# Window attention: mask, maximum and copy of the scores in one VectorE instruction

## The chip, the cores and the metric

The kernel runs on one core of a Trainium2 chip. A core has a matrix engine (TensorE, PE in the profile, with its weight loads as PEld), a vector engine (VectorE, DVE), a scalar engine (ScalarE, ACT), a general engine (GpSimd, POOL) and queues that issue transfers (here SyncE's, SP). Each engine runs its own instructions in order, and they wait for each other by semaphores. Matrix products go to PSUM, the rest lives in SBUF. The metric is the device time of one execution in microseconds.

## The reference, cut to what matters

The program is one step of a small backbone of two layers on 256 context tokens and 1024 latent tokens. The change lies in the first layer's attention: 16 query heads in 4 groups that share keys and values, 64 dimensions a head. For the latent tokens each block of 128 queries sees the three blocks of 128 keys around it (two at either end), a mask that cuts this to +-128 tokens, 256 cached keys that are not masked, and a learned logit per head, the sink, which counts in the softmax but has no value:

```python
valid = (jnp.abs(qpos[:, None] - kpos[None, :]) <= WINDOW) & (kpos >= 0)[None, :] & (kpos < T)[None, :]
s_loc = jnp.einsum('bqhgd,bkhd->bhgqk', qi, ki, preferred_element_type=F32) * scale
s_loc = jnp.where(valid, s_loc, NEG_INF)
s_ctx = jnp.einsum('bqhgd,bkhd->bhgqk', qi, ck, preferred_element_type=F32) * scale
p = jax.nn.softmax(jnp.concatenate([s_loc, s_ctx, sink_b], axis=-1), axis=-1)
p_loc = p[..., :3 * BLOCK].astype(v.dtype)
p_ctx = p[..., 3 * BLOCK:3 * BLOCK + L].astype(v.dtype)
```

The context tokens attend to all 256 context keys and the sink, without a mask.

## The kernel before, in words

The attention stage handles 40 groups: 4 head groups, each with the latent blocks 0 to 7 and the context blocks 8 and 9, in the order 0, 1, 2, 8, 3, 4, 5, 9, 6, 7. A group has four heads, so there are 160 heads and blocks, 128 of them with a window. The instructions stand in the order in which the code issues them. `Attention.run` counts ticks. In one tick it normalises (`normal`) the pair of heads scored two ticks ago, takes the maximum (`peak`) of the head scored in the tick before, turns and splits one block of 128 keys of four finished heads (`turn`, `split`), multiplies the block turned before by the values (`weighted`), takes the exponential (`exp`), does a piece of other work (`extra`: projections, later the output product, tiles `mm`), and issues the score products (`scores`) of the next head. Scores are issued at least seven ticks less the head's number ahead of the group's first `turn`.

Scores go to a tile D of two PSUM banks, of which there are two. Columns 0 to 511 hold the window, right-aligned (`off` is its first column: 128 inside, 256 in blocks 0 and 7, 512 for context blocks, which have none), 512 to 767 the cached keys. Keys are held as a high and a low part, `att_kh` and `att_kl`; each part takes one product per piece. For a window a third product adds the mask: a 128x128 identity times the triangular masks, both kept in bf16 in a tile `mbf`, which is filled when startup ends. The queries' high and low part lie one above the other in `att_q`.

`peak` (L1368 and L1369) copies the head's sink to column 768 of D and takes the maximum of the columns from `off` to 768, negated, into `att_nm`. `exp` (L1374) reads D from PSUM, writes the tile `att_p` (`att_pp` for context blocks) in SBUF and adds up the denominators, `att_den`. `normal` (L1380 and L1383) inverts these and scales `att_p` on POOL. `turn` transposes `att_p` on TensorE (L123), `split` (L1394 and L1395) makes a high part `att_ph` on ScalarE and a low part `att_pl` on VectorE, and `weighted` multiplies both by `att_v` into V. `a_sinks` loads the sinks; `LR` loads the masks into `K.small` at startup.

All matrix products stand at L119 in the profile, transposes at L123, loads at L154.

Of the kernel before, what the change touches and what calls it, by code (L numbers as in the profile page):

```python
# [11 lines left out]
F32 = mybir.dt.float32  # L12
F32R = mybir.dt.float32r
BF16 = mybir.dt.bfloat16
AF = mybir.ActivationFunctionType
ALU = mybir.AluOpType
AX = mybir.AxisListType
# [34 lines left out]
def _rope_tables(n_tok, width, grid_w=64, base=10000.0):  # L52
    half = width // 4
    f32 = np.float32
    freqs = np.power(f32(base), -(np.arange(half, dtype=f32) / f32(half))).astype(f32)
    t = np.arange(n_tok)
    pos = [(t // grid_w).astype(f32), (t % grid_w).astype(f32)]
    cos = np.zeros((width, n_tok), f32)
    sin = np.zeros((width, n_tok), f32)
    for ax in range(2):  # L60
        ang = (pos[ax][None, :] * freqs[:, None]).astype(f32)
        c, s = np.cos(ang), np.sin(ang)
        r = ax * 2 * half
        cos[r:r + half] = c
        cos[r + half:r + 2 * half] = c
        sin[r:r + half] = -s
        sin[r + half:r + 2 * half] = s
    reps = 128 // width
    return np.tile(cos, (reps, 1)), np.tile(sin, (reps, 1))


def _constants():
    f32 = np.float32
    ca, sa = _rope_tables(TS, 64)
    cc, sc = _rope_tables(TS, 32)
    p = np.arange(128)[:, None]
    f = np.arange(128)[None, :]
    eye = (p == f).astype(f32)
    m_f = np.where(p <= f, 0, NEG).astype(f32)
    m_b = np.where(p >= f, 0, NEG).astype(f32)  # L80
    w_lo = np.where(f >= p, 0, NEG).astype(f32)
    w_hi = np.where(f <= p, 0, NEG).astype(f32)
    rst = np.ones((128, T), f32)
    rst[0:32, 0::128] = 0
    rst[32:64, 127::128] = 0
    return {
        "k_small": np.concatenate([eye, m_f, m_b, m_f, w_lo, w_hi], axis=1),
        "k_ropea": np.concatenate([ca, sa], axis=1),
        "k_ropec": np.concatenate([cc, sc], axis=1),
        "k_rst": rst,  # L90
    }
# [68 lines left out]
def body(tc, I, O, dbg=None, stop_at=None):  # L160
    K = Kern(tc, I, O, dbg)
    with ExitStack() as ctx:
        K.const = ctx.enter_context(tc.tile_pool(name="const", bufs=1))
        K.dram = ctx.enter_context(tc.tile_pool(name="dram", bufs=1, space=DRAM))
        K.left = lambda n: tc.alloc_tile_pool(name=n, bufs=1, side="left", reuse_waits="tile")
        K.right = lambda n: tc.alloc_tile_pool(name=n, bufs=1, side="right", reuse_waits="tile")
        K.set_psum(S=6, T=2)
        setup_consts(K)
        layer_ab(K)
        layer_c(K)  # L170
        K.set_psum()
# [35 lines left out]
def setup_consts(K):  # L207
    nc, c = K.nc, K.const
    K.ident = c.tile([128, 128], F32, tag="ident", name="ident")
    K.small = c.tile([128, 5, 128], F32, tag="small", name="small")  # L210
    K.mbf = c.tile([128, 3, 128], BF16, tag="mbf", name="mbf")
    unit = c.tile([128, 5], F32, tag="unit", name="unit")
    nc.vector.memset(unit, 0.0)
    nc.vector.memset(unit[:, 1:2], 1.0)
    K.vpad = unit[:, 1:5].rearrange("p (a e) -> p a e", a=2)
    K.sel = [unit[:, 1:3], unit[:, 0:2]]
    K.mhalf = c.tile([128, 1], F32, tag="mhalf", name="mhalf")
    nc.vector.memset(K.mhalf, -0.5)


class Startup:
# [21 lines left out]
    def run(self, order, room):  # L243
        K, nc = self.K, self.K.nc
        self.G = room
        self.by = dict(a=nc.scalar, v=nc.vector, p=nc.gpsimd)
        K.flow = self
        for token in order.split():
            name, at, by = re.fullmatch(r"([A-Za-z]+)(\d*)([avp]?)", token).groups()
            getattr(self, name)(*[int(a) for a in at], *by)  # L250
        while self.kept or self.last:
            if not self.kept:
                self.kept, self.last = self.last, []
            self.kept.pop(0)()
        K.flow = None
        nc.vector.tensor_copy(K.mbf[:, 0, :], K.ident)
        nc.vector.tensor_copy(K.mbf[:, 1:3, :], K.small[:, 3:5, :])

    def later(self, f, n):
        self.kept.append(f)  # L260
# [638 lines left out]
def layer_ab(K):  # L899
# [90 lines left out]
    with K.tc.manual_schedule():  # L990
        K.pairs = True
        beside_memory(K, bp, dense, 23, 230)
        K.pairs, K.spread = False, True
        bp.release()
        gp.release()
        K.set_psum(D=2, mm=3, V=1)
        ap = left("att")
        a_sinks(K, ap)
        K.rpool.release()
        stage = right("raw")  # L1000
        steps = beside_attention(K, ap, dense, place_wout(K, hp, w, wt, stage, [8, 9, 10, 11, 12, 13], 3),
                                 release)
# [187 lines left out]
def a_sinks(K, ap):  # L1190
    nc = K.nc
    K.sink = ap.tile([128, 16], F32, tag="sink", name="sink")
    K.dma(K.sink, K.I["sink_a"].to_broadcast([128, 16]))


def a_proj(K, wp, g):
# [119 lines left out]
class Group:  # L1316
# [27 lines left out]
    def scores(self, h):  # L1344
        K, (kh, kl), b, off, c0 = self.A.K, self.A.kk, self.b, self.off, self.c0
        S = self.D[h] = K.t(K.psum["D"], [128, 1024], F32, "D")
        q = self.q[:, h, :]
        if b < 8:
            K.mm(S[:, off:512], q, kh[:, self.k0:self.k1], True, False)
            K.mm(S[:, off:512], q, kl[:, self.k0:self.k1], False, False)  # L1350
            if b == 0:
                K.mm(S[:, 384:512], K.mbf[:, 0, :], K.mbf[:, 2, :], False, True)
            elif b == 7:
                K.mm(S[:, off:off + 128], K.mbf[:, 0, :], K.mbf[:, 1, :], False, True)
            else:
                ends = S[:, 0:512].rearrange("p (a f) -> p a f", a=2)[:, :, 128:256]
                K.mm(ends, K.mbf[:, 0, :], K.mbf[:, 1:3, :], False, True)
        K.mm(S[:, 512:768], q, kh[:, c0:c0 + 256], True, False)
        K.mm(S[:, 512:768], q, kl[:, c0:c0 + 256], False, True)

    def peak(self, h):
        K, ap, S = self.A.K, self.A.ap, self.D[h]
        if h % 2 == 0:
            P = K.t(ap, [128, 2, 648], F32, "att_p", 5) if self.b < 8 else K.t(ap, [128, 2, 264], F32, "att_pp", 2)
            self.P[h // 2] = (P, K.t(ap, [128, 2], F32, "att_nm", 4),
                              K.t(ap, [128, 2], F32, "att_den", 4))
        i = 4 * self.g + h
        K.nc.vector.tensor_copy(S[:, 768:769], K.sink[:, i:i + 1])  # L1368
        K.nc.vector.tensor_reduce(self.P[h // 2][1][:, h % 2:h % 2 + 1], S[:, self.off:769], AX.X, ALU.max, negate=True)  # L1369

    def exp(self, h):
        P, nm, den = self.P[h // 2]
        i = slice(h % 2, h % 2 + 1)
        self.A.K.nc.scalar.activation(P[:, h % 2, 0:self.w + 1], self.D[h][:, self.off:769], AF.Exp,  # L1374
                                      bias=nm[:, i], accum_out=den[:, i])

    def normal(self, pr):
        P, _, den = self.P[pr]
# [1230 lines left out]
```

## Time and profile before

| | us |
|---|---|
| median of 3 runs | 2569.25 |
| lowest and highest run | 2566.27 and 2574.26 |
| profiled execution, device time | 2568.26 |
| profiled execution, span of its instructions | 2566.5 |
| first to last score product of the stage | 1030.4 to 1426.0 |
| in that stage: TensorE, VectorE, ScalarE, GpSimd busy | 391.57, 300.24, 272.48, 213.28 |

Line numbers are those of the kernel before; from the first lines of the change on, those of the changed kernel differ by a few. In a row of groups the operands stand as out<-in with partitions x elements, then the count, the busy time and the mean of one, then the engine's idle time before them with what ended it. In rows in order of time the first number is the start, the second the duration. Matmuls overlap, and their ends are modelled, so durations of TensorE's rows cannot be added up.

### The profile page before, as it was taken

Reading aid. Unit: us, or ns where it says so; the run is one execution under the profiler, and the core shown is the slowest. Engines: PE = TensorE matmul, PEld = TensorE weight load, DVE = VectorE, ACT = ScalarE, POOL = GpSimd, SP = SyncE. Lnnn points to the kernel's source line nnn. Section 1 sums busy time; section 2 is a strip of 40 time slices with the busy share of each in tenths; the row PEclk is TensorE's granted clock in tenths of the full one; section 3 lists DMA queues with packets and bytes.
Section 4 is the critical chain, followed back from the end, with each engine's and each line's share of the span. In section 5 each row is a group of like instructions: output and inputs, shape, how many; then the busy total and the mean of one; then the engine's idle time right before and its main releaser. Section 6 shows DMA issues by size and latency. Waiting matters only on the chain.

```text
span 2566.5 us, 48614 instructions
## 1 busy us (share of the span) xinstructions
PE 2526.6 (98%) x16482; PEld 2245.1 (87%) x16482; DVE 1700.2 (66%) x3925; ACT 1438.6 (56%) x3665; POOL 1131.6 (44%) x1512
## 2 busy tenths in 40 slices
PE   8999999999999999999999999999999999999998
PEld 6898998998998888878888888898899999999887
DVE  6643655756657575687777456436888888888754
ACT  6423534535534432577666433234888888888842
POOL 6222333333325344366554543135555545555732
PEclk9999999999999999999999999999999999999999
DMA  7665576566667574465443554433211111111334
GB/s 266 212 181 175 156 219 189 170 201 186 191 207 223 171 222 147 116 175 155 126 130 94 168 164 161 126 82 110 67 35 31 39 30 41 33 32 35 115 99 133
DMA packets 338954, 347.20 MB, mean 135 GB/s; under 512 B 36409, under 2 KB 281838, under 8 KB 338450
## 3 DMA queue, kind: packets, MB, share of 16 engines
q1 hardware_dynamic: 338706, 344.10, 43.9%
q8 instruction: 131, 2.15, 0.3%
q14 instruction: 117, 0.96, 0.1%
HBM read 233.49 MB, written 110.50 MB: 134 GB/s over the span
## 4 chain that ended last, share of the span: by engine, by line
PE 87%; DVE 3%; ACT 2%; issue 1%; POOL 1%; DMA 1%; SPq 0%; POOLq 0%; DVEq 0%; ACTq 0%
PE mm L119 36%; PE S L119 29%; PE V L119 9%; PE T L123 7%; PE D L119 3%; PE mm L123 3%; PE T L119 1%; DVE cpl L2549 0%; DVE cmx L2499 0%; POOL w L1070 0%; DVE att_pl L1395 0%; DMA out_new_cache_a_k<-scr 0%; ACT att_ph L1394 0%; DVE att_nm L1369 0%; ACT cPa L2501 0%
## 5 line engine op out<-in xcount | busy, mean ns | idle before, releaser
L585 POOL TENSOR_TENSOR wl<-wf,wh 128x256 fp32r<-128x256 f32 (+2 forms) x272 | 223.0, 846 | 483.6 <-ACT wh L584 399.6
L119 PE MATMUL mm<-hTh,wh 128*128 128x512 f32 (+1 forms) x912 | 329.2, 361 | 0.9 <-DVE scr L870 0.9
L119 PE MATMUL mm<-hTh,wl 128*128 128x512 f32 (+1 forms) x912 | 324.7, 356 | 0.0
L119 PE MATMUL mm<-hTl,wh 128*128 128x512 f32 (+1 forms) x912 | 324.1, 355 | 0.0
L119 PE MATMUL S<-cK,cQ 96*128 96x512 f32 (+3 forms) x1248 | 298.2, 364 | 0.8 <-ACT cPa L2501 0.7
L2549 DVE TENSOR_TENSOR cpl<-T,cph 128x512 fp32r<-128x512 f32 x336 | 228.8, 685 | 45.2 <-ACT cph L2548 41.8
L119 PEld LDWEIGHTS S<-cK,cQ 96*128 96x128 f32 (+1 forms) x1248 | 193.5, 189 | 22.5 <-ACT cPa L2501 2.8
L2548 ACT CAST cph<-T 128x512 fp32r<-128x512 f32 x336 | 192.6, 590 | 30.2 <-PE T L123 21.2
L119 PEld LDWEIGHTS mm<-hTh,wl 128*128 128x128 f32 x912 | 171.5, 188 | 27.0
L119 PEld LDWEIGHTS mm<-hTh,wh 128*128 128x128 f32 x912 | 171.5, 188 | 23.8 <-DVE scr L870 1.1
L119 PEld LDWEIGHTS mm<-hTl,wh 128*128 128x128 f32 x912 | 171.7, 188 | 23.2
L2499 DVE TENSOR_REDUCE cmx<-S 128x1 f32<-128x512 f32 x256 | 173.2, 682 | 19.5 <-PE S L119 18.4
L1394 ACT CAST att_ph<-mm 128x512 fp32r<-128x512 f32 x168 | 98.6, 587 | 93.2 <-PE mm L123 89.9
L2480 POOL TENSOR_SCALAR cPa<-cPa,cst 128x512 f32<-128x512 f32 x128 | 99.0, 773 | 108.1 <-DVE cst L2477 91.4
L1395 DVE TENSOR_TENSOR att_pl<-mm,att_ph 128x512 fp32r<-128x512 f32 x168 | 115.8, 689 | 35.7 <-ACT att_ph L1394 30.9
L119 PE MATMUL mm<-wh,hTh 128*128 128x256 f32 x480 | 135.5, 282 | 0.0
L119 PE MATMUL mm<-wl,hTh 128*128 128x256 f32 x480 | 134.9, 281 | 0.0
L119 PE MATMUL mm<-wh,hTl 128*128 128x256 f32 x480 | 134.5, 280 | 0.0
L1383 POOL TENSOR_SCALAR att_p<-att_p,att_den 128x640 f32<-128x640 f32 (+1 forms) x128 | 97.9, 779 | 79.4 <-DVE att_den L1380 31.4
L584 ACT CAST wh<-wf 128x256 fp32r<-128x256 f32 (+2 forms) x272 | 96.0, 409 | 60.3 <-DMA wf<-in_w_in_c 29.3
L119 PE MATMUL V<-cph,cV 128*128 128x256 f32 x440 | 118.1, 289 | 1.9 <-ACT cph L2548 1.9
L1369 DVE TENSOR_REDUCE att_nm<-D 128x1 f32<-128x641 f32 (+2 forms) x160 | 114.9, 718 | 5.5
(488 smaller groups left out, 7938.9 us busy)
## 6 DMA issues: line engine op xcount, KB each, us to landing
wf<-in_w_in_ab SPq DMA_DIRECT2D x120, 256.0 KB, 3.8
in<-in SPq DMA_DIRECT2D x40, 514.0 KB, 3.5
in<-in SPq DMA_DIRECT2D x32, 386.0 KB, 3.8
mw<-in_w_mod SPq DMA_DIRECT2D x48, 256.0 KB, 4.7
in<-scr SPq DMA_DIRECT2D x40, 258.0 KB, 3.6
o_x<-y SPq DMA_DIRECT2D x20, 512.0 KB, 3.5
xin<-in_k_wmod SPq DMA_DIRECT2D x16, 512.0 KB, 7.9
in<-cx SPq DMA_DIRECT2D x32, 256.0 KB, 3.5
```

The costliest lines, as they stand in the source:

```text
L119: return self.nc.tensor.matmul(out, lhsT, rhs, start=start, stop=stop)
L123: self.nc.tensor.transpose(out, in_, self.ident[:p, :p])
L584: K.nc.scalar.copy(wh, wf[:, k])
L585: K.nc.gpsimd.tensor_sub(wl, wf[:, k], wh.bitcast(F32))
L1369: K.nc.vector.tensor_reduce(self.P[h // 2][1][:, h % 2:h % 2 + 1], S[:, self.off:769], AX.X, ALU.max, negate=True)
L1383: nc.gpsimd.tensor_scalar(pv, pv, den[:, i:i + 1], 1.0, ALU.mult, ALU.mult)
L1394: K.nc.scalar.copy(ph, self.T)
L1395: K.nc.vector.tensor_sub(pl, self.T, ph.bitcast(F32))
L2480: nc.gpsimd.tensor_scalar(pv, pv, wt[:, c:c + 1], rd, ALU.mult, ALU.mult)
L2499: nc.vector.tensor_reduce(mx[:, b, c:c + 1], S, AX.X, ALU.max, negate=True)
L2548: nc.scalar.copy(ph, T_)
L2549: nc.vector.tensor_sub(pl, T_, ph.bitcast(F32))
```

## The change

The mask product on TensorE and its bf16 tile go away. A mask in f32, laid out as the scores are (two triangles and zeros in five blocks of 128 columns), is loaded once into SBUF when the stage begins, and the sinks are negated there. In `peak` one VectorE instruction reads the scores from PSUM and the mask from SBUF, writes minus their sum to `att_p`, and keeps the minimum of these, starting from the negated sink; a second instruction of the pair stores that minimum in `att_nm`. The negated sinks are copied into the column behind the scores, for two heads at a time. `exp` then works on `att_p` in place, with a factor of -1. Block 7 has its two window blocks in another place than the others, so it reads the mask in two pieces. Context blocks go through the same instruction with the zero part of the mask.

```diff
         "k_small": np.concatenate([eye, m_f, m_b, m_f, w_lo, w_hi], axis=1),
+        "k_mask": np.concatenate([w_lo, 0 * eye, w_hi, 0 * eye, 0 * eye], axis=1),
...
-    K.mbf = c.tile([128, 3, 128], BF16, tag="mbf", name="mbf")
...
-        nc.vector.tensor_copy(K.mbf[:, 0, :], K.ident)
-        nc.vector.tensor_copy(K.mbf[:, 1:3, :], K.small[:, 3:5, :])
...
     K.dma(K.sink, K.I["sink_a"].to_broadcast([128, 16]))
+    K.mask = ap.tile([128, 768], F32, tag="mask", name="mask")
+    K.dma(K.mask[:, 0:640], K.I["k_mask"])
+    nc.vector.tensor_scalar(K.sink, K.sink, -1.0, None, ALU.mult)
...
             K.mm(S[:, off:512], q, kh[:, self.k0:self.k1], True, False)
-            K.mm(S[:, off:512], q, kl[:, self.k0:self.k1], False, False)
-            if b == 0:
-                K.mm(S[:, 384:512], K.mbf[:, 0, :], K.mbf[:, 2, :], False, True)
-            elif b == 7:
-                K.mm(S[:, off:off + 128], K.mbf[:, 0, :], K.mbf[:, 1, :], False, True)
-            else:
-                ends = S[:, 0:512].rearrange("p (a f) -> p a f", a=2)[:, :, 128:256]
-                K.mm(ends, K.mbf[:, 0, :], K.mbf[:, 1:3, :], False, True)
+            K.mm(S[:, off:512], q, kl[:, self.k0:self.k1], False, True)
...
-        i = 4 * self.g + h
-        K.nc.vector.tensor_copy(S[:, 768:769], K.sink[:, i:i + 1])
-        K.nc.vector.tensor_reduce(self.P[h // 2][1][:, h % 2:h % 2 + 1], S[:, self.off:769], AX.X, ALU.max, negate=True)
+        P, nm, _ = self.P[h // 2]
+        w, off, i = self.w, self.off, 4 * self.g + h
+        if h % 2 == 0:
+            K.nc.vector.tensor_copy(P[:, :, w:w + 1], K.sink[:, i:i + 2].unsqueeze(2))
+        out, src, mask = P[:, h % 2, 0:w], S[:, off:768], K.mask[:, 640 - w:640]
+        if self.b == 7:
+            out, src = [t.rearrange("p (a f) -> p a f", a=2) for t in (out, src)]
+            mask = K.mask.rearrange("p (a f) -> p a f", a=2)[:, :, 0:256]
+        K.nc.vector.tensor_tensor_reduce(out, src, mask, -1.0, K.sink[:, i:i + 1], ALU.add, ALU.min, nm[:, h % 2:h % 2 + 1])
...
-        self.A.K.nc.scalar.activation(P[:, h % 2, 0:self.w + 1], self.D[h][:, self.off:769], AF.Exp,
-                                      bias=nm[:, i], accum_out=den[:, i])
+        pv = P[:, h % 2, 0:self.w + 1]
+        self.A.K.nc.scalar.activation(pv, pv, AF.Exp, bias=nm[:, i], scale=-1.0, accum_out=den[:, i])
```

The order of the remaining instructions stays. On TensorE, at the scores of one head with a full window (D is its score tile, `mm_14119` the turned tile that follows), there stood before:

```order
L119 MATMUL D_14111<-att_kh,att_q_13915 128x384
L119 MATMUL D_14111<-att_kl,att_q_13915 128x384
L119 LDWEIGHTS mbf
L119 MATMUL D_14111<-mbf 128x2x128
L119 MATMUL D_14111<-att_kh,att_q_13915 128x256
L119 MATMUL D_14111<-att_kl,att_q_13915 128x256
L123 MATMUL mm_14119<-ident,att_p_13919 128x128 x2
```

and in the changed kernel:

```order
L120 MATMUL D_14101<-att_kh,att_q_13914 128x384
L120 MATMUL D_14101<-att_kl,att_q_13914 128x384
L120 MATMUL D_14101<-att_kh,att_q_13914 128x256
L120 MATMUL D_14101<-att_kl,att_q_13914 128x256
L124 MATMUL mm_14107<-ident,att_p_13918 128x128 x2
```

The mask's weight load and product are gone, and the products of the cached keys follow at once.

On VectorE, at the peaks of a pair of heads between two subtractions of `split`, with what each waits for in brackets (PE, DVE, Activation and Pool are the engines, VectorE itself among them), there stood before:

```order
L1368 COPY D_14439<-sink 128x1 [waits PE_49]
L1369 TENSOR_REDUCE att_nm_14451<-D_14439 128x1 [waits DVE_49]
L1395 TENSOR_TENSOR att_pl_14461<-mm_14455,att_ph_14460 128x512 [waits Activation_49]
L1368 COPY D_14470<-sink 128x1 [waits PE_49]
L1369 TENSOR_REDUCE att_nm_14451<-D_14470 128x1 [waits DVE_49]
L1395 TENSOR_TENSOR att_pl_14484<-mm_14478,att_ph_14483 128x512 [waits Activation_49]
L1380 RECIPROCAL att_den_14452<-att_den_14452 128x2 [waits Activation_49,Pool_49]
```

and in the changed kernel:

```order
L1364 COPY att_p_14426<-sink 128x2
L1369 ISA att_p_14426,att_nm_14427<-D_14416,mask,sink 128x640 [waits PE_49]
L1369 ISA att_nm_14427 128x1
L1395 TENSOR_TENSOR att_pl_14437<-mm_14431,att_ph_14436 128x512 [waits DVE_49,Activation_49]
L1369 ISA att_p_14426,att_nm_14427<-D_14446,mask,sink 128x640 [waits PE_49]
L1369 ISA att_nm_14427 128x1
L1395 TENSOR_TENSOR att_pl_14458<-mm_14452,att_ph_14457 128x512 [waits DVE_49,Activation_49]
L1380 RECIPROCAL att_den_14428<-att_den_14428 128x2 [waits Activation_49,Pool_49]
```

The copy of the sinks stands once for two heads and waits for nothing; the combined instruction takes the maximum's place, with the store of the minimum behind it as an instruction of its own; and the wait of VectorE for itself has moved from the maximum to the subtraction at L1395.

## The prediction

> **What bounds the kernel now.** I read the page first, then the stage that the change touches, then the chain of waits inside it, then TensorE's own waits, and last the order of single instructions.
>
> ```profile
> span 2566.5 us, 48614 instructions
> PE 2526.6 (98%) x16482; PEld 2245.1 (87%) x16482; DVE 1700.2 (66%) x3925; ACT 1438.6 (56%) x3665; POOL 1131.6 (44%) x1512
> ```
>
> TensorE is busy almost everywhere, but that figure is modelled, so it proves nothing alone. The changed code runs from the first score product at 1030.4 us to the last at 1426.0. The windows view gives that stretch (length, then busy time and instructions of PE, weight load, DVE, ACT, POOL, then clock, DMA share, GB/s), and the chain of waits, cut to 1200 to 1215 us inside it, says who sets the pace:
>
> ```profile
> 1030.40:1426.00 395.60, 391.57 (x2351) 329.76 (x2350) 300.24 (x660) 272.48 (x624) 213.28 (x268) 1.00 0.46 132
> ```
>
> ```profile
> by line: PE mm L119 38.6%; PE V L119 22.2%; PE D L119 20.7%; PE mm L123 18.9%
> ```
>
> The chain consists of TensorE alone: no other engine appears in it. DVE is second with 300.2 of 395.6 us, 76%, at a granted clock of 1.00. TensorE's waits between 1030 and 1430 us are few (total us, times, longest):
>
> ```profile
> PE D L119 <- ACT att_p L1374: 2.1, 2, 1.3
> PE V L119 <- DVE att_pl L1395: 0.8, 2, 0.6
> PE mm L123 <- DVE att_pl L1395: 0.5, 2, 0.3
> PE mm L123 <- POOL att_p L1383: 0.4, 1, 0.4
> ```
>
> Together 3.8 us, 1% of the stage. So what leaves TensorE's queue here shortens the program, as long as DVE keeps up.
>
> **What leaves TensorE.** One mask product per head and block with a window: 4 groups x 8 blocks x 4 heads = 128, each a weight load and a matmul. Its price is not its own duration (0.28 us below), because matmuls overlap; it is how much later the next starts. TensorE's rows in order of time (start, us):
>
> ```profile
> 1201.88 0.28 PE L119 MATMUL D<-att_kh,att_q 128*128 128x256 f32 x1
> ...
> 1202.12 0.60 PE L123 MATMUL mm<-ident,att_p 128*128 128x128 f32 x4
> ...
> 1203.71 0.34 PE L119 MATMUL D<-att_kh,att_q 128*128 128x384 f32 x1
> ...
> 1204.06 0.28 PE L119 MATMUL D<-mbf 128*128 128x256 bf16 x1
> 1204.10 0.36 PE L119 MATMUL D<-att_kh,att_q 128*128 128x256 f32 x1
> 1204.31 0.28 PE L119 MATMUL D<-att_kl,att_q 128*128 128x256 f32 x1
> 1204.42 0.60 PE L123 MATMUL mm<-ident,att_p 128*128 128x128 f32 x4
> ```
>
> A head without a mask needs two 256-column products: 1202.12 - 1201.88 = 0.24 us from first start to the next work. A masked head takes 1204.42 - 1203.71 = 0.71. Its two 384-column products take 1204.06 - 1203.71 = 0.35, its two 256-column products 0.24 as before, so the mask costs 0.71 - 0.35 - 0.24 = 0.12 us. It shows mostly one place late: the mask row is followed after 0.04 us, but the product behind it then holds its place for 0.21 instead of about 0.11. For the edge blocks, whose mask has 128 columns, the first and last rows of one head are
>
> ```profile
> 1425.05 0.28 PE L119 MATMUL D<-att_kh,att_q 128*128 128x256 f32 x1
> ...
> 1425.65 0.60 PE L123 MATMUL mm<-ident,att_p 128*128 128x128 f32 x4
> ```
>
> 0.60 - 0.24 - 0.24 = 0.12 again. Sum: 128 x 0.12 = 15.4 us off TensorE. Bounds: 128 x 0.04 = 5.1 if only the direct distance counts, 128 x 0.28 = 35.8 by full durations. I take 15.4, since whole heads were measured from end to end.
>
> **What VectorE gets.** Gone are 160 one-column copies and 160 maxima. New are 160 combined instructions (scores from PSUM plus mask from SBUF, negated, written to SBUF, running minimum), 160 separate reads of the minimum, and 80 sink copies for two heads each. The groups that price them (count | busy us, mean ns):
>
> ```profile
> L1369 DVE TENSOR_REDUCE att_nm<-D 128x1 f32<-128x641 f32 x96 | 79.2, 825 | 3.3
> L1369 DVE TENSOR_REDUCE att_nm<-D 128x1 f32<-128x513 f32 x32 | 22.1, 692 | 1.1
> L1369 DVE TENSOR_REDUCE att_nm<-D 128x1 f32<-128x257 f32 x32 | 13.6, 425 | 1.1
> L1368 DVE COPY D<-sink 128x1 f32<-128x1 f32 x160 | 25.4, 158 | 29.7 <-PE D L119 26.6 <-PE mm L123 0.2
> L1395 DVE TENSOR_TENSOR att_pl<-mm,att_ph 128x512 fp32r<-128x512 f32 x163 | 112.4, 689 | 30.4 <-ACT att_ph L1394 25.6
> L1704 DVE TENSOR_TENSOR scr<-mm,scr 128x256 fp32r<-128x256 f32 x30 | 12.7, 423 | 14.4 <-ACT scr L1703 14.1
> L1374 ACT ACTIVATION_READ_ACCUMULATOR att_p<-D,att_nm 128x1 f32 x128 | 24.7, 193 | 0.0
> ```
>
> ```profile
> L1786 DVE COPY Cs<-n x8: 163/331/925, 201.5 to 783.0; 128x4 f32<-128x4 f32 x8
> ```
>
> Removed: 79.2 + 22.1 + 13.6 + 25.4 = 140.3 us. The combined instruction is not in this trace. Its nearest rows are the two-stream subtractions with one input in PSUM: 689 ns for 512 columns, 423 for 256, so 1.04 ns a column and 822 for 640. That gives 96 x 0.822 + 32 x 0.689 + 32 x 0.423 = 114.5 us, the same as the maxima that it replaces (114.9); a running maximum is evidently not dearer than an element each step. The read of the minimum lies between nothing and 193 ns (ScalarE's read of its sum); I take VectorE's own row for one column, the copy's 158: 25.3 us (0 to 30.9). The sink copies are 80 x 0.158 = 12.6, at most 80 x 0.925 = 74 by the slowest small copy (L1786: shortest, median and longest ns). Added 152.4, so VectorE gets +12 us (-13 to +79): 312 of 395.6 - 15.4 = 380.2 us, 82%. That cover hides it; without the cover it would cost its 12 us.
>
> [...]
>
> One wait is new: the subtraction at L1395, whose result the next product V needs, now also waits for VectorE's own read before it; before, only the maximum waited so, for its copy. Without such a wait the rows overlap:
>
> ```profile
> 1205.71 0.83 DVE L1369 TENSOR_REDUCE att_nm<-D 128x1 f32<-128x641 f32 x1
> 1206.45 0.68 DVE L1395 TENSOR_TENSOR att_pl<-mm,att_ph 128x512 fp32r<-128x512 f32 x1
> ```
>
> The maximum ends at 1206.54, so 0.09 us of overlap goes; the overlap that copy and maximum lacked comes back. Queued behind are the next reciprocal and peak, for which POOL and ACT wait, seven ticks ahead of their use. Taken as zero.
>
> **What ScalarE and the queues get.** The exponential reads SBUF instead of PSUM. Casts of one size show the difference:
>
> ```profile
> L1394 ACT CAST att_ph<-mm 128x512 fp32r<-128x512 f32 x163 | 95.7, 587 | 87.9 <-PE mm L123 84.6 <-PE V L119 1.8
> L1043 ACT CAST hh<-wraw 128x512 fp32r<-128x512 f32 x20 | 12.3, 614 | 0.3 <-DMA wraw<-in_w_out_ab 0.2
> ```
>
> 27 ns x 160 = 4.3 us on an engine that is busy 272 of 396 us: hidden. In return the score bank is free after VectorE instead of after ScalarE, which may remove the 2.1 us that D waited for att_p; I set that against new waits for VectorE, sum zero. SP issues one more DMA (the mask, 320 KB) behind the sinks, and VectorE negates the sinks:
>
> ```profile
> 1017.17 0.41 SPq L154 DMA_DIRECT2D sink<-in_sink_a  x1
> 1022.82 0.69 DVE L895 SCALAR_TENSOR_TENSOR scr<-scr,mm 128x512 f32<-128x512 f32 x1 [6.37 <-ACT scr L894]
> att_v<-vhl SPq DMA_DIRECT2D x8, 256.0 KB, 3.8
> ```
>
> VectorE idles 6.37 us there, more than a transfer's 3.8, so its new wait for the sinks is covered; all later loads of the stage slip by about half a microsecond of issue, while the first score product comes 13 us after the sinks. The mask is there by about 1022 and is first read after 1030. Zero. The two casts dropped at startup (under 1 us of VectorE) are zero too.
>
> **Sum.** Span 2566.5 - 15.4 = 2551.1. Around the span lie 2568.26 - 2566.5 = 1.8 us, so 2552.9; the median of the runs, 2569.25, is 1.0 above the profiled execution: 2553.9.
>
> **Rivals.**
> *Hidden load.* The mask product may sit in the shadow of weight loads, and only the 0.04 us distance is won: 128 x 0.04 = 5.1, so 2564. For it speaks that the weight load overlaps; against it that the neighbour's 0.21 us shrinks to 0.11 in every unmasked head.
> *VectorE late in bursts.* The means hide ticks in which two att_o rows, a subtraction and a peak meet. If the copies lean to the 925 ns end, VectorE comes to 379 of 380 us and TensorE waits for att_pl: half the gain or more goes, 2561 to 2569. Against it: only 1.3 us of TensorE's waits name att_pl today.
> *The combined instruction is slow, and VectorE becomes the bound (other side).* An instruction with a running result is in the trace, and it is slow; another with two streams is not (min/median/max ns):
>
> ```profile
> L1586 DVE TENSOR_TENSOR_SCAN gM<-LF,m,LI x2: 2339/2340/2342, 123.3 to 125.6; 4x1024 f32<-4x1024 f32 x2
> L1586 DVE TENSOR_TENSOR_SCAN gM<-LF,LI x2: 1046/1047/1048, 136.7 to 137.8; 4x256 f32<-4x256 f32 x2
> ...
> L1687 DVE SCALAR_TENSOR_TENSOR cx<-scr,cx x48: 408/684/1227, 78.3 to 686.0; 128x512 f32<-128x512 f32 x32, 128x256 f32<-128x256 f32 x16
> ```
>
> The scan takes (2340 - 1047) / 768 = 1.68 ns a column plus 616, so 1.69, 1.48 and 1.05 us for 640, 512 and 256 columns: 243 us in place of 114.5, VectorE at 441 us, 45 more than the stage has now, hence 2614. The point where this decides is VectorE over 395.6 us, 83 above my sum, or 0.52 us on each of the 160, a mean of 1.24 us in place of 0.72: about 2569 at that point. Against it: the maximum, also a running result, goes at 1.04 ns a column. [...]
>
> **How the numbers follow.** Forecast 72%, bursts 12%, hidden load 8%, slow instruction 8%. Two runs differ from no change only beyond about 0.3%, 7.7 us, so the borders are 2561.5 and 2577. Faster: the forecast and a sixth of the bursts, 0.74; same: the rest of the bursts and hidden load, 0.18; slower 0.08. The low end, 2546, is the sum with the 3.8 us of waits gone and 0.15 instead of 0.12 us a product; the high end, 2566, takes in hidden load and most bursts.
>
> **What would show it.** Right: no mbf rows; masked heads of 0.59 us from first D start to the transposes; L1369 at about 822/689/423 ns; the read under 0.2; the stage near 380 us with a chain of TensorE alone. Wrong: L1369 near 1.5 us, DVE in the chain, or TensorE waits for att_pl of several microseconds.

## The result: less than half of the forecast gain, and the profile after

| | before | changed |
|---|---|---|
| median, us (20 runs each) | 2570.8 | 2564.35 |
| span of the profiled execution, us | 2566.5 | 2560.1 |
| ratio, 95% interval | | 0.9974 (0.9968 to 0.9981) |

The kernel became faster by 6.5 us (4.9 to 8.2 by the interval); the forecast was 15.4. The median, 2564.35, lies near the top of the forecast's range of 2546 to 2566, which was put there for the rivals; the sum that the prediction argued for is 2553.9. The page of the changed kernel begins so:

```profile
span 2560.1 us, 48511 instructions
PE 2515.9 (98%) x16354; PEld 2246.2 (88%) x16354; DVE 1699.3 (66%) x4004; ACT 1437.2 (56%) x3665; POOL 1128.9 (44%) x1512
```

TensorE has 128 matmuls fewer, 16354 in place of 16482: all mask products are gone. The windows view from the first to the last score product:

```profile
1030.17:1418.00 387.83, 377.95 (x2218) 330.09 (x2217) 299.25 (x739) 272.04 (x623) 212.21 (x268) 1.00 0.47 135
```

The stage takes 387.8 us where 380.2 were forecast and 395.6 were measured before. VectorE is busy 299.3 us, less than the 312 of the forecast and no more than before (300.2). Yet TensorE waits more. Its waits in the changed kernel, first for the matmuls, then for the weight loads (total us, times, longest):

```profile
PE V L120 <- DVE att_pl L1395: 2.8, 7, 0.9
PE D L120 <- DMA att_q<-ql: 2.1, 2, 1.3
PE V L120 <- DVE att_o L1413: 1.3, 2, 0.8
...
PEld V L120 <- DVE att_pl L1395: 7.5, 15, 1.2
PEld V L120 <- ACT att_ph L1394: 2.3, 4, 0.9
PEld mm L124 <- POOL att_p L1383: 2.0, 4, 0.6
```

Where they lie is told by cutting both traces at three places (windows view, columns as above). The kernel before, then the changed one:

```profile
1030.00:1104.00 74.00, 73.91 (x450) 62.42 (x449) 52.87 (x120) 48.14 (x112) 31.70 (x43) 1.00 0.44 128
1104.00:1175.00 71.00, 67.12 (x420) 55.30 (x418) 54.48 (x123) 56.88 (x130) 47.53 (x55) 1.00 0.65 190
1175.00:1400.00 225.00, 224.93 (x1332) 190.37 (x1332) 173.93 (x377) 150.02 (x343) 120.83 (x153) 1.00 0.42 119
```

```profile
1030.00:1104.00 74.00, 71.97 (x429) 63.03 (x428) 52.22 (x136) 48.86 (x114) 31.66 (x43) 1.00 0.44 128
1104.00:1175.00 71.00, 64.12 (x389) 54.53 (x388) 56.81 (x135) 55.32 (x127) 46.92 (x55) 1.00 0.66 188
1175.00:1400.00 225.00, 224.04 (x1302) 196.79 (x1300) 175.02 (x432) 155.27 (x357) 123.76 (x157) 1.00 0.42 121
```

From 1175 us on, TensorE has 0.1 us of gaps before the change and 1.0 after it. From 1030 to 1104 us it has 0.1 before and 2.0 after, 1.3 of these in one wait for `att_q`. Between 1104 and 1175 it has 3.9 us of them before (71.00 - 67.12) and 6.9 after. Already before the change ScalarE was busy 80% and GpSimd 67% of the time there, against 67% and 54% from 1175 to 1400. The same can be read as progress: how much earlier a block's first score product comes, counted from the first score product of the kernel. The rows for the first block, the sixteenth (the first after 1175 us) and the last, before and then changed:

```profile
1030.35 0.29 PE L119 MATMUL D<-att_kh,att_q 128*128 128x256 f32 x1
...
1175.05 0.42 PE L119 MATMUL D<-att_kh,att_q 128*128 128x384 f32 x1
...
1417.77 0.28 PE L119 MATMUL D<-att_kh,att_q 128*128 128x256 f32 x1
```

```profile
1030.17 0.29 PE L120 MATMUL D<-att_kh,att_q 128*128 128x256 f32 x1
...
1175.78 0.34 PE L120 MATMUL D<-att_kh,att_q 128*128 128x384 f32 x1
...
1410.74 0.28 PE L120 MATMUL D<-att_kh,att_q 128*128 128x256 f32 x1
```

Up to the sixteenth block the changed kernel has lost time: 144.70 us before, 145.61 after, a gain of -0.9. From there to the last block it takes 234.96 in place of 242.72, a gain of 7.8 for 76 mask products, 9.1 by the forecast's price. So most of the forecast comes there, and the loss sits at the start of the stage. Every kernel below was read in this way:

| block's first score product, at us before | 1041.3 | 1106.3 | 1175.0 | 1235.0 | 1417.8 |
|---|---|---|---|---|---|
| mask products passed x 0.12 | 0.5 | 2.9 | 5.8 | 8.2 | 14.9 |
| changed kernel, gain in us | -0.8 | 0.7 | -0.9 | 0.5 | 6.8 |
| TensorE's part alone (e1) | -0.9 | 0.4 | 0.8 | 1.4 | 8.2 |
| VectorE's part alone (e2) | -0.5 | -0.4 | -2.8 | -2.7 | -2.5 |
| the same, sinks as a maximum (e12) | -0.4 | -0.3 | 0.2 | 0.3 | 0.6 |
| changed, sinks as a maximum (e3) | -0.2 | 1.3 | 2.9 | 3.6 | 10.6 |
| changed, no copy (e4) | -0.7 | 0.9 | 2.1 | 3.6 | 10.6 |
| changed, queries earlier (e5) | 0.1 | 1.5 | -0.1 | 2.0 | 8.3 |
| TensorE's part, queries earlier (e6) | -0.1 | 1.1 | 2.7 | 4.7 | 11.6 |
| changed, both edits (e7) | 0.4 | 2.0 | 3.7 | 4.8 | 11.5 |
| before, queries earlier (e8) | -0.6 | -0.6 | -0.4 | -0.4 | -0.4 |

Each row is one profiled execution. Steps of half a microsecond at single places should not be read for more than they are; the pattern over all rows can be. What lies ahead of the stage took 1028.5 to 1032.6 us in all the kernels here, and what follows its last head 1139 to 1148 (before the change 1141.5, after it 1142.4), without an order that the edits explain; that is why device times and gains over the stage differ by some microseconds.

The costs of the new work, by groups (count | busy us, mean ns | idle before):

```profile
L1369 DVE CUSTOM_DVE_ANT_0 att_p<-D,mask,sink 128x640 f32<-128x640 f32 x96 | 84.5, 880 | 11.7 <-PE D L120 10.7
L1364 DVE COPY att_p<-sink 128x2 f32<-128x2 f32 x64 | 18.4, 288 | 0.2
L1369 DVE CUSTOM_DVE_ANT_0 att_pp<-D,mask,sink 128x256 f32<-128x256 f32 x32 | 15.4, 480 | 3.1 <-PE D L120 2.6
L1369 DVE DVE_READ_ACCUMULATOR2_ANT att_nm<- 128x1 f32 x160 | 13.2, 83 | 0.0
L1369 DVE CUSTOM_DVE_ANT_1 att_p<-D,mask,sink 128x512 f32<-128x512 f32 x16 | 12.0, 748 | 2.0 <-PE D L120 1.7
L1369 DVE CUSTOM_DVE_ANT_0 att_p<-D,mask,sink 128x512 f32<-128x512 f32 x16 | 11.9, 748 | 1.9 <-PE D L120 1.7
L1364 DVE COPY att_pp<-sink 128x2 f32<-128x2 f32 x16 | 3.3, 203 | 0.0
```

```profile
L1364 DVE COPY att_p<-sink x64: 147/149/2125, 1033.0 to 1416.4; 128x2 f32<-128x2 f32 x64
```

The combined instruction takes 57 to 59 ns more than estimated at each width, its read 83 ns in place of 158. Most copies take 149 ns, but one takes 2125. It stands in this stretch of the trace (start, us):

```profile
1163.89 2.55 POOL L1042 TENSOR_TENSOR hl<-wraw,hh 128x512 fp32r<-128x512 f32 x2
1164.39 2.12 DVE L1364 COPY att_p<-sink 128x2 f32<-128x2 f32 x1
...
1166.54 0.88 DVE L1369 CUSTOM_DVE_ANT_0 att_p<-D,mask,sink 128x640 f32<-128x640 f32 x1
...
1167.35 0.69 DVE L1395 TENSOR_TENSOR att_pl<-mm,att_ph 128x512 fp32r<-128x512 f32 x1
...
1168.09 0.50 PE L120 MATMUL V<-att_pl,att_v 128*128 128x512 f32 x1 [0.94 <-DVE att_pl L1395]
```

GpSimd subtracts two rows of weights from 1163.89 to 1166.44. The copy, two elements wide, begins inside that time and ends with it, at 1166.51. Behind it on VectorE stand the combined instruction and the subtraction for `att_pl`, and TensorE waits 0.94 us for the latter. The other long copies look alike. Of the 80 copies 22 began while a GpSimd instruction ran; 19 of these take 189 ns or more, and 18 of the 19 ended 24 to 29 ns after that instruction did. Only the one shown here lasted through the next as well. The 58 other copies take 170 ns at most.

### The profile page after: what moved, and what is told of

Read it like the earlier page. It is cut to its first block, busy times and chain, and to the rows that moved or that the text cites. A ratio compares the mean times of both kernels' runs of the same rounds, so it can differ in the third digit from the quotient of the medians.

```text
span 2560.1 us, 48511 instructions
## 1 busy us (share of the span) xinstructions
PE 2515.9 (98%) x16354; PEld 2246.2 (88%) x16354; DVE 1699.3 (66%) x4004; ACT 1437.2 (56%) x3665; POOL 1128.9 (44%) x1512
## 4 chain that ended last, share of the span: by engine, by line
PE 83%; DVE 3%; issue 2%; ACT 2%; DMA 2%; POOL 1%; SPq 1%; POOLq 0%; DVEq 0%; ACTq 0%
PE mm L120 34%; PE S L120 28%; PE V L120 8%; PE T L124 7%; PE mm L124 2%; PE D L120 2%; SPq L155 1%; PE T L120 1%; DMA y<-w 0%; POOL w L1117 0%; DMA att_q<-ql 0%; DMA o_a<-aT 0%; ACT att_ph L1394 0%; DVE att_pl L1395 0%; POOL att_p L1383 0%
## 5 line engine op out<-in xcount | busy, mean ns | idle before, releaser
L1395 DVE TENSOR_TENSOR att_pl<-mm,att_ph 128x512 fp32r<-128x512 f32 x168 | 116.0, 690 | 46.2 <-ACT att_ph L1394 44.0
L1375 ACT ACTIVATE att_p<-att_p,att_nm 128x641 f32<-128x641 f32 (+1 forms) x128 | 103.4, 808 | 42.3 <-DVE att_nm L1369 35.4
```

The lines of the kernel that those rows point to most:

```text
L1375: self.A.K.nc.scalar.activation(pv, pv, AF.Exp, bias=nm[:, i], scale=-1.0, accum_out=den[:, i])
L1395: K.nc.vector.tensor_sub(pl, self.T, ph.bitcast(F32))
```

## The experiments

Each kernel ran 5 or 11 times, beside the kernel before on the same chip. The ratios come from all of these runs and can differ from the quotient of two medians by about 0.001. Medians and ratios:

| | us | ratio to before, 95% interval |
|---|---|---|
| e1, TensorE's part alone | 2559.06 | 0.9957 (0.9943 to 0.9970) |
| e2, VectorE's part alone | 2574.40 | 1.0016 (1.0007 to 1.0025) |
| e3, sinks as a maximum | 2561.47 | 0.9968 (0.9956 to 0.9981) |
| e4, no copy | 2561.24 | 0.9964 (0.9951 to 0.9976) |
| e5, queries earlier | 2561.62 | 0.9966 (0.9952 to 0.9979) |
| e6, TensorE's part, queries earlier | 2557.74 | 0.9952 (0.9940 to 0.9965) |
| e7, sinks as a maximum, queries earlier | 2559.39 | 0.9957 (0.9944 to 0.9969) |
| e8, before, queries earlier | 2569.09 | 0.9993 (0.9984 to 1.0002) |
| e9, before, no split | 2570.01 | 0.9997 (0.9988 to 1.0006) |
| e10, changed, no split | 2561.01 | 0.9959 (0.9946 to 0.9973) |
| e11, both edits, no split | 2556.76 | 0.9947 (0.9935 to 0.9960) |
| e12, VectorE's part, sinks as a maximum | 2570.06 | 1.0005 (0.9996 to 1.0014) |
| e13, before, queries earlier, no split | 2566.03 | 0.9988 (0.9979 to 0.9997) |
| e14, both edits, casts only | 2554.43 | 0.9949 (0.9936 to 0.9961) |
| e15, both edits, subtractions only | 2555.48 | 0.9950 (0.9937 to 0.9962) |

**e1 and e2: the two halves of the change.** e1 is the kernel before without the third product:

```diff
-            K.mm(S[:, off:512], q, kl[:, self.k0:self.k1], False, False)
-            if b == 0:
...
+            K.mm(S[:, off:512], q, kl[:, self.k0:self.k1], False, True)
```

> The kernel before without the mask product; the masks are left out of the scores, and VectorE's copies, maxima and everything else stay. Theory A (the product is worth 15.4 us, and what is missing in the changed kernel was lost to VectorE's new instructions): the whole gain appears, ratio about 0.994 to 0.995, first to last score product about 380 us. Theory B (the gain itself is given back, because the loads of att_q and the chain of transposes, att_ph and att_pl keep their own pace when TensorE goes faster): the ratio stays near the changed kernel's 0.9974, the stage near 387 us, and TensorE waits more than the 3.8 us of before without VectorE having got anything to do.

e2 is the changed kernel with the mask products put back:

> The changed kernel with the mask product put back on TensorE, so the mask is added twice (still minus infinity where it cuts). All of VectorE's new work, none of TensorE's relief. Theory A: VectorE's part alone costs what is missing, 6 to 9 us: ratio 1.002 to 1.0035. Theory B: TensorE has its old slack again, VectorE's part is hidden: ratio 0.999 to 1.001.

e1 gains 11.1 us and e2 loses 4.3; together that is a gain of 6.8, close to the change's 6.5. So VectorE's part does cost something, and TensorE's part alone does not give 15.4 either. Over the stage this is plainer: e1 takes 386.5 us from the first score product to the last, theory B's 387 and not theory A's 380, and by the table of progress it gains 8.2 of 14.9 us. So 6.7 us are missing there without any of VectorE's new work. In the same table e2 loses 2.8 us before 1175 us and nothing in the 240 us behind it. Each theory holds in part.

**e3, e4 and e12: the copies of the sinks.** e3 writes the two sinks as a maximum over one element each (called one-port copy in the expectations, which is a name only: no run shows a port), e4 leaves the copies and with them the sinks in the denominators out:

```diff
-            K.nc.vector.tensor_copy(P[:, :, w:w + 1], K.sink[:, i:i + 2].unsqueeze(2))
+            K.nc.vector.tensor_reduce(P[:, :, w], K.sink[:, i:i + 2].unsqueeze(2), AX.X, ALU.max)
```

> The changed kernel with each of the 80 sink copies written as a maximum over one element: the same values, and an instruction of the kind that showed steady durations in every row. Theory A1 (within A: the copies that GpSimd holds up, 31 of 80 with a mean of 465 ns and up to 2.1 us, make VectorE late): all 80 take about 150 ns, VectorE's sum falls by 10 us, TensorE's waits for att_pl fall from 10.3 us (PE and PEld) to about the 3.8 of before, ratio 0.995 to 0.996. Theory A2 (the combined instruction's 57 ns over the estimate and the subtraction's wait do it) and theory B: durations fall, the time stays near 0.997.

> The changed kernel without the sink copies; the exponential covers the scores alone, so the sink is left out of the denominators (it still starts the minimum). The most that anything done to the copies can give. Theory A1: 0.994 to 0.996, a little below the kernel with one-port copies. A2 and B: near 0.997.

The row of the new form in e3 (shortest, median, longest ns):

```profile
L1364 DVE TENSOR_REDUCE att_p<-sink x64: 132/136/158, 1032.2 to 1412.2; 128x2 f32<-128x2 f32 x64
```

The longest is 158 ns in place of 2125, although 20 of the 80 lie wholly inside a GpSimd instruction; these take 133 to 157 ns. Over the stage e3 and e4 gain 10.6 us each against 6.8: 3.8 us come back, 3.2 of them in e3 between the blocks at 1106.3 and 1175.0 us, and a maximum over one element is as good as no copy at all. (In device time the difference to the changed kernel is 2 to 3 us, within the intervals, and the ratios 0.9968 and 0.9964 miss what theory A1 forecast, so the stage has to decide.) Where the plain copies of the changed kernel lose time, by groups from 1104 to 1175 us and then from 1175 on:

```profile
L1364 DVE COPY att_p<-sink 128x2 f32<-128x2 f32 x12 | 6.6, 549 | 0.0
L1364 DVE COPY att_pp<-sink 128x2 f32<-128x2 f32 x2 | 0.5, 248 | 0.0
...
L1364 DVE COPY att_p<-sink 128x2 f32<-128x2 f32 x40 | 9.7, 242 | 0.2
L1364 DVE COPY att_pp<-sink 128x2 f32<-128x2 f32 x10 | 1.7, 165 | 0.0
```

Over 149 ns each, the 14 copies of the first stretch lose 5.0 us, the 50 behind it 3.9; there it hardly matters, since from 1235 us on the changed kernel gains 6.3 of 6.7 us.

e12 puts the same edit into e2:

> VectorE's part alone (mask products kept on TensorE), with the one-port copy of the sinks. With the plain copy this kernel was slower by 4 us (1.0016) and lost 2.5 us between the first and the last score product. Theory E (of VectorE's new work only the copies held up by GpSimd cost anything; the dearer combined instruction and its read are hidden): no loss over the stage (0 to 0.5 us), ratio 0.9995 to 1.0005. Theory F (the dearer combined instruction delays the low parts att_pl as well): 1 to 3 us of loss stay, ratio 1.0005 to 1.0012.

The loss over the stage is gone (a gain of 0.6), and the ratio falls from 1.0016 to 1.0005, with an interval that holds 1 (the two intervals overlap, so the verdict rests on the stage). Theory E stands: the held-up copies made the loss, and the dearer combined instruction and its read cost nothing on balance.

**e5 to e8: loads of the queries.** Beside the copies the waits name `att_q`. In the changed kernel:

```profile
1229.87 0.60 SPq L155 DMA_DIRECT2D att_q<-qh  x1
1230.53 0.61 SPq L155 DMA_DIRECT2D att_q<-ql  x1
...
1234.30 0.41 PE L120 MATMUL D<-att_kh,att_q 128*128 128x384 f32 x1 [0.77 <-DMA att_q<-ql]
```

Before, this product started at 1234.97, after a load issued at 1230.92. The load is asked for when the block ahead starts its scores; before the change the 40 loads of `qh` and the 40 of `ql` took 3.4 and 3.6 us in the median from issue to landing, and in the rows above `ql` ended TensorE's wait 3.77 us after its issue. The edit asks one block earlier, into three buffers:

```diff
-            at(self.G[n - 1].s0 + 1 if n else 0, G.load)
+            at(self.G[n - 2].s0 + 1 if n > 1 else n, G.load)
...
-        self.q = K.t(self.A.ap, [128, 4, 128], F32R, "att_q", 2)
+        self.q = K.t(self.A.ap, [128, 4, 128], F32R, "att_q", 3)
```

> The changed kernel, with the queries of each block (att_q) loaded one block earlier, into three buffers in place of two (the score rows att_p are padded to 644 in place of 648 columns, to make room). Theory A (VectorE's new work alone gives the gain back): the waits for att_q are only where TensorE would have waited anyway, so the ratio stays at the change's 0.9974, 2564. Theory B (the loads of the stage were hidden by just the time that the mask products took, so part of the gain returns as waits for att_q): the 3.3 us that TensorE and its weight loads waited for att_q in the changed kernel go, and little else: ratio 0.9961, 2560.5 to 2562, no wait of TensorE on att_q over 0.3 us.

> The kernel before without its mask products (the masks are left out of the scores), VectorE's work as before, and att_q loaded one block earlier into three buffers. Without the earlier load this kernel gained 11 of the 15.4 us (0.9957). Theory A: the missing 4 us are noise of the order of work, ratio 0.9957 again. Theory B: the 3.5 us of waits for att_q go, ratio 0.9943, gain 14 to 15 us.

> The changed kernel with both edits: att_q one block earlier, and the copies of the sinks as a maximum over one element each. Theory A: as with the copy's edit alone, 0.9968. Theory B: the two parts add up, 3 us from the copies and 3 from the loads: ratio 0.995, 2557 to 2559; what is left of the 15.4 us is the dearer combined instruction.

> The kernel before, mask products and all, with att_q loaded one block earlier into three buffers. Both theories: no change (0.9995 to 1.0005), since TensorE waited only 0.3 us for att_q there. If it gains over 0.1%, the earlier load is an improvement of its own and says nothing on the change.

TensorE's waits for matmuls in e1 began with the first row below; in e6 they begin with the second, and `att_q` is not among them:

```profile
PE D L119 <- DMA att_q<-ql: 3.5, 3, 1.6
...
PE D L119 <- ACT att_p L1367: 2.5, 3, 1.1
```

Over the stage the earlier load gives 1.5 us (e5 against the changed kernel), 3.4 (e6 against e1) and 0.9 (e7 against e3); before the change it gives nothing (-0.4). By the ratios the four pairs differ by 1.3 to 2.8 us in the same direction, each within the intervals; e8, which gains nothing over the stage, is among them with 1.8, so device times do not settle this. The ratios of e5, e6 and e7 all stay short of theory B's (0.9961, 0.9943 and 0.995). So theory B holds in kind, the waits are real and go, but beside the other losses of the changed kernel they were worth only about 1 us, not the 3 that I expected. e7 is the fastest version of the changed kernel that leaves nothing out: its 0.9957 stands against the change's 0.9974. And e7 reaches what e6 reaches (11.5 and 11.6), though e6 has none of VectorE's change: with the copies mended, VectorE's part costs nothing on balance. It is a balance, because VectorE's part also gives something: the 2.5 us for which D waits for `att_p` in e6 are gone in e7, where the score bank is free after VectorE (D waits 0.3 us there, for `att_nm`), and a cost of about that size may stand against them. About 3.3 of the 14.9 us are still missing in both.

**e9 to e15: what else happens between 1104 and 1175 us.** There the chain of waits of the kernel before is not TensorE's alone. Its shares by line, from 1119 to 1160 us, and then from 1175 to 1410:

```profile
by line: issue 11.9%; DMA wraw<-in_w_out_ab 8.8%; DVE att_nm L1369 7.8%; PE mm L119 7.4%; POOL att_p L1383 7.2%; SPq L154 6.8%; DVE att_pl L1395 6.3%; PE mm L123 6.0%; PE V L119 5.9%; ACT att_p L1374 5.0%; PE D L119 5.0%; ACT att_ph L1394 4
...
by line: PE mm L119 38.2%; PE D L119 23.6%; PE V L119 19.3%; PE mm L123 18.3%; DVE att_pl L1395 0.3%; ACT att_ph L1394 0.3%; issue 0.1%; ACTq L1394 0.0%
```

In this stretch 16 half rows of output weights (`wraw`) are loaded and split in two, beside the attention's own work. GpSimd's costliest group there, in the changed kernel:

```profile
L1042 POOL TENSOR_TENSOR hl<-wraw,hh 128x512 fp32r<-128x512 f32 x16 | 20.6, 1292 | 20.0 <-ACT hh L1041 20.0
```

The edit leaves this splitting out, and fills both halves by transfers:

```diff
-        wf = K.t(stage, [128, 512], F32, "wraw", 4)
-        K.dma(wf, src[k * 128:(k + 1) * 128, sl])
-        K.later(partial(split, [t[:, sl] for t in wt[at]], wf), lag)
+        for t in wt[at]:
+            K.dma(t[:, sl], K.d["qh"][0][0:128, 0:512])
```

> The kernel before, but the output weights that are brought in during this stage (wraw) are no longer cast by ScalarE and split by GpSimd (hl): both halves are filled by a transfer of other data, so the products with them are wrong numbers at the same cost. It is the base for the next two. Theory C (between about 1104 and 1175 us these splits, not TensorE, set the pace, so the mask products there are worth nothing, and GpSimd's splits hold up the copies of the sinks): TensorE's waits of the stage fall from 5.8 to under 3 us, 2565 to 2568. Theory D (the softmax chain itself is too slow there, with or without the splits): 2569 to 2571, the waits as before.

> The changed kernel with the same edit. To be compared with the kernel before with that edit, over the time from the first to the last score product. Theory C: the change now gains 11 to 13 us there in place of 6.8 (what is left are waits for att_q and copies held up by GpSimd's other work), device time 2553 to 2557. Theory D: it gains about 7 us as without the edit, 2560 to 2564.

> The changed kernel with the one-port copy, att_q one block earlier, and the same edit. Theory C: against the kernel before with that edit the gain over the stage is 14 to 15.4 us, the whole of the mask products, 2550 to 2554. Theory D: 11 to 12 us as without the edit, 2556 to 2559.

The time from the first score product to that of the last block is 387.2 us in e9, 377.4 in e10 and 372.4 in e11: a gain of 9.8 for the change (6.8 with the splits) and 14.7 for the change with both edits. The 9.8 lies between what the two theories forecast (11 to 13, and about 7), and e10's device time, 2561.0, is theory D's. The copies of e10 between 1104 and 1175 us show one reason for the 9.8; without GpSimd's subtractions the longest is 171 ns there, where it was 2125 with them:

```profile
L1363 DVE COPY att_p<-sink x12: 147/150/171, 1110.6 to 1168.6; 128x2 f32<-128x2 f32 x12
```

But the 14.7 is too good. Theory C expected e9's waits to fall, and they did not; its trace shows a wait that the kernel before does not have at this block, probably made by the extra transfers in the queue (this load was issued at 1135.16 us there, and at 1132.88 before the change):

```profile
1138.53 0.41 PE L119 MATMUL D<-att_kh,att_q 128*128 128x384 f32 x1 [1.47 <-DMA att_q<-ql]
```

So three more kernels followed: a base without that wait, and the two halves of the split apart.

> The kernel before with its mask products, with the weight splits left out as in the runs without splits, and with att_q loaded one block earlier. The former base without splits waited 1.5 us for an att_q that its own extra transfers had made late; here that wait should be gone, which makes this the cleaner base for the kernel with both edits and no splits (372.4 us from the first score product to that of the last block). If the splits cost the kernel before nothing: 387 us again, and the full gain of 14.7 stands. If they cost it as much as that wait hid: 385.5 to 386, 2568 to 2569, and the gain without splits is only 13.2 to 13.7, so that the stretch from 1104 to 1175 us has another cause in part.

> The changed kernel with the one-port copy and att_q one block earlier; of the splits of the output weights only ScalarE's cast is left, the low half is filled by a transfer of other data in place of GpSimd's subtraction. If GpSimd's subtractions are what the shorter kernel runs into: 372.5 to 373 us over the stage as without any split, 2556 to 2557. If ScalarE's casts are: 375.5 to 376 as with the splits, 2558.5 to 2560.

> The same, but GpSimd's subtraction is left and the high half is filled by a transfer of other data in place of ScalarE's cast. If GpSimd's subtractions are the cause: 375.5 to 376 us over the stage, 2558.5 to 2560. If ScalarE's casts are: 372.5 to 373, 2556 to 2557. If both matter a little: both kernels near 374.

From the first score product to that of the last block, with queries earlier in all of them:

| | mask products in place | change and both edits | gain of 14.9 |
|---|---|---|---|
| with the splits | 387.8 (e8) | 375.9 (e7) | 11.9 |
| ScalarE's casts only | | 374.2 (e14) | |
| GpSimd's subtractions only | | 373.7 (e15) | |
| without the splits | 385.9 (e13) | 372.4 (e11) | 13.4 |

The splits cost the kernel with the mask products 1.9 us and the one without them 3.5. So 1.5 of the 3 us that are missing fall to them, and the other 1.5 are missing without them too. Theory C explains half. (The device time of e13, 2566.0, lies below both of its forecasts; the 385.9 us over the stage are the second one.) Neither half of the split is the culprit alone: e14 and e15 lie between, 1.3 to 1.8 us above e11 and 1.7 to 2.2 below e7. The device times of e7, e11, e14 and e15 (0.9947 to 0.9957) are too close to rank. In device time e11 stands to e13 as 0.9947 to 0.9988, 10.5 us, with intervals that allow 13. What is left in e11 from 1104 to 1175 us (windows view, columns as above):

```profile
1104.00:1175.00 71.00, 68.02 (x422) 59.56 (x421) 57.12 (x148) 51.23 (x119) 31.66 (x44) 1.00 0.87 256
```

GpSimd is half idle, VectorE busy 80% and ScalarE 72%, and 3.0 us of TensorE's time are empty. Its matmuls wait there for `att_pl` (1.0 us), `o_ah` (0.9), `att_ph` (0.6) and the combined instruction (0.2). No run takes these apart, so what sets them stays open.

## Where the prediction was right and where it was wrong, point by point

The price of the mask product was right; two steps behind it failed. The prediction let every 0.12 us shorten the program, on a chain of waits that it had read from 15 us of the stage, and it took the new copies on VectorE as hidden under a mean.

**Price of the mask product: right.** A masked head in the changed kernel, from its first score product to the transposes behind it:

```profile
1203.64 0.34 PE L120 MATMUL D<-att_kh,att_q 128*128 128x384 f32 x1
...
1204.23 0.60 PE L124 MATMUL mm<-ident,att_p 128*128 128x128 f32 x4
```

That is 0.59 us, as forecast, and from 1235 us to the last block e7 gains 11.5 - 4.8 = 6.7 us for 56 products, 0.12 each. The rival of the hidden load is out.

**"So what leaves TensorE's queue here shortens the program": wrong for a fifth of the stage.** I showed the chain from 1200 to 1215 us, where it is TensorE alone, and took it for the stage. From 1119 to 1160 us the same view names VectorE, ScalarE, GpSimd and transfers. "Together 3.8 us" of waits was true and no protection: nearly all of TensorE's gaps lay together in one stretch, and a shorter TensorE lengthens them there. In e1, which gives VectorE nothing new to do, they grow from 3.9 to 5.4 us between 1104 and 1175 us, and 6.7 of 14.9 us are missing over the stage. With the copies and loads mended, about 3 us stay missing (e7), nearly all of them by the block after the one at 1175.0 us; half of them fall to the splits of the weights, and the cause of the other half is open.

**"That cover hides it": the term that was put at nothing.** The sum for VectorE came out high (312 us; 299 measured), the dearer combined instruction costs nothing on balance (e12), and still 3.8 us were lost through the copies (e3), 3.2 of them between 1106 and 1175 us. I had the right row (163 to 925 ns for a small copy) and priced each copy at the short end, then set the total against a mean of 82%. What counts is not the copies' sum over the stage but how long they are held where TensorE has no slack: the 5.0 us over 149 ns each from 1104 to 1175 us cost most of the 3.8, the 3.9 us behind it almost nothing. The longest copy does not make the loss alone: in its block the changed kernel's lag behind e3 grows from 3.1 to 3.9 us. In the trace of the changed kernel 18 copies that began during a GpSimd instruction ended 24 to 29 ns after it did, and one after the end of the next. The maximum over one element that stands in their place in e3 took 136 ns in the median and 158 at most, and 133 to 157 inside GpSimd's instructions. No run shows why the two differ.

**The self-wait of `att_pl`: rightly zero.** In the rows above the subtraction starts at 1167.35, 0.07 us before the combined instruction ends at 1167.42. The overlap is still there, and as often: where this subtraction follows a peak it starts before the peak's end in 47 of 154 cases, 46 of 154 before the change.

**"Zero" for the queues: wrong by about 1 us.** One more transfer for the mask did no harm: e1 has none and waits for `att_q` as well. What I left out is that `att_q` is asked for only one block ahead, with almost no slack, and that a faster TensorE arrives before it: in the rows above the product came 4.05 us after the issue of its load before the change (1234.97 - 1230.92), and 3.77 us after it, at the end of a wait of 0.77, in the changed kernel. The 1 us is what the earlier load gives beside the other losses; in TensorE's part alone it gives 3.4 (e6 against e1). The other zero here, the score bank that comes free earlier against VectorE's new waits, was about right as a balance (e7 against e6).

**ScalarE's 27 ns: about right.** For 641 columns the exponential takes 835 ns in place of 799. No run takes this apart from the rest of VectorE's part, which with the copies mended loses nothing (e12):

```profile
L1375 ACT ACTIVATE att_p<-att_p,att_nm 128x641 f32<-128x641 f32 x96 | 80.1, 835 | 31.5 <-DVE att_nm L1369 25.0 <-POOL att_pp L1383 4.0 <-POOL o_al L1480 1.6
```

**Rivals.** The rival of late bursts, 2561 to 2569, came nearest, and the sign named for it came too: TensorE's matmuls wait 2.8 us for `att_pl` and its weight loads 7.5. But it is only part of what happened. Its condition, copies at the long end that fill VectorE to 379 us, did not come (most took 149 ns; 299 us), and the copies account for 3.8 of the 8.1 us; that the time fell into its range is in part luck. Its 12% were too few, because I had argued from the small waits on `att_pl` before the change. The slow combined instruction did not come: 880, 748 and 480 ns, far from 1.69, 1.48 and 1.05 us.

The account over the stage, in us and in this order of edits: 14.9 expected, 6.8 seen; 3.8 back by the sinks as a maximum (e3), 0.9 more by earlier queries (e7, 11.5; 11.9 against e8), 1.5 more without the splits (e11 against e13), and 1.5 left open. Each term is a difference of single profiled executions, good to about half a microsecond (e8, which should show nothing, differs by 0.4), and another order divides the sum otherwise.

## What to carry to other kernels

Before a saving on the busiest engine is counted in full, read the chain and that engine's gaps stretch by stretch: here 3.9 us of the gaps lay together between 1104 and 1175 us, where the chain named other engines too, and e1 was short of the expected gain by 5.0 us at the block at 1175.0 us. A tiny instruction that another engine can hold up (149 ns in the median here, 2125 at most) is to be priced by its long rows and by what stands behind it, not by its median; here two-element copies cost 3.8 of the 8.1 us that were missing, and writing them as reductions brought those back. An engine that gets faster also moves up on transfers asked for a fixed number of steps ahead: look at the slack between landing and first use (here a product that came 4.05 us after the issue of its load came after 3.77 in the changed kernel, 0.77 of them spent waiting).

## What the runs showed of the hardware that was not expected

A VectorE copy of two elements between SBUF tiles took 149 ns in the median of the changed kernel, and 170 at most where it did not begin during a GpSimd instruction. Of the 22 that did, 19 took 189 ns or more; 18 of these ended 24 to 29 ns after that instruction, and one, at 2125 ns, after the next. A maximum over one element with the same operands took 132 to 158 ns in e3, in all 80 cases. The combined instruction takes (880 - 480) / (640 - 256) = 1.04 ns a column plus 213 ns, against 156 ns beside the columns for the plain subtraction (689 - 512 x 1.04), and its separate read of the minimum only 83 ns. The exponential from SBUF took 32 to 36 ns more than from PSUM at all three widths (513 against 481, 727 against 693, 835 against 799).
